# Matmuls without a reader in TensorE's idle places, and modulation sums queued behind named VectorE sums

## The chip, the core and the metric

The kernel runs on one core of a Trainium2 chip. The metric is the device time of one execution in microseconds (us); less is better. Times are medians over several runs. A profile comes from one execution of its own; all positions below are us from the start of its span. Engines: PE is TensorE (PEld its weight loads), DVE VectorE, ACT ScalarE, POOL GpSimd, SP the queue that issues most DMAs.

## What is computed

One layer of a diffusion backbone over 1,024 latent and 128 context tokens of width 1,024, all in float32. Cut to what matters here:

```python
def modulation(cvec, w_ada, b_ada):          # for c and for c_ctx
    m = silu(cvec) @ w_ada + b_ada           # 6 vectors of 1024
    return split(m, 6)                       # sh1, sc1, ga1, sh2, sc2, ga2

h = rmsnorm(x, g1) * (1 + sc1) + sh1
...                                          # in-projection, Fourier mixer, attention, merge -> m
x = x + ga1 * (m @ w_out)
h = rmsnorm(x, g2) * (1 + sc2) + sh2
x = x + ga2 * (square(relu(h @ w_ff1)) @ w_ff2)
y = rmsnorm(x, final_g)
```

## The kernel before

Each float32 matrix product is made of three faster passes: an operand is cast to a rounded high part (ScalarE, `whi`) and the rest is its low part (VectorE, `wlo`, by `sub`), and high x high, high x low and low x high are summed in a PSUM bank. Nine tiles of 128 tokens (eight latent ones, and tile 8 for the context) go through these stages: the head (load x, norms, 72 transposes to channel-major, the modulation vectors of the first norm), the in-projection, Fourier mixer and attention, the output projection (`w_out`, in three groups of three tiles), FF1, FF2. The two feed-forward products use a scheme of seven products (numbered 1 to 7) on halves of the operands instead of eight; `prod` makes one of them.

FF1 runs in 16 blocks `p` of 256 hidden columns. In a block, `step_p1`, `step_p4`, `step_p2`, `step_ctx` (context tile), `step_p6`, `step_p7`, `step_p5` and, a block later, `step_p3` are TensorE's products; `ev_p1`, `ev_p2`, `ev_p6`, `ev_p7`, `ev_c2`, `ev_p3` read them out with sums on VectorE and relu and square on ScalarE. `step_p2` goes on in the bank that `ev_p1` must have read before it. `ff1_load` fetches the next block's weights on SP, `ff1_u` and `ff1_sums` split and add them.

The seam between the last `w_out` group (tiles 6, 7, 8) and FF1 is ordered by hand for TensorE, VectorE, ScalarE and GpSimd (`manual_schedule`, from `ff1_load(0)` to `man.close()`). There block 0 is done in two parts, `RA` (three quarters of the latent tokens, 384 columns) and `RB` (128 columns), because the last latent tiles and the context tile come late: `unit_end` closes the last `w_out` sums, `fin_a` adds them to x, `fin_b` makes the norm's scale, `fin_c` transposes the scaled tile and applies the modulation, `t_hi` and `t_lo` write the operand's halves. The context tile's operand is `cth` (ScalarE) and `ctl` (VectorE).

Everything outside that seam is ordered by a planner that simulates the engines with its own costs. It may also put instructions from behind the seam between those of the seam, and it orders SP's queue throughout.

The modulation vectors of the second norm and gate are made by VectorE and ScalarE beside other work: `mod_step` takes one step of `msteps`: a load of 128 KB of `w_ada` on SP and two VectorE products or accumulations (lines 309 and 311), or, at the end of a block of 256 columns, a transpose and a reduction (320, 321). 40 steps (`MOD_LATE`) are left for FF1. During FF1 the loads alternate between two slots in `zh(15, 2)`, which the seam uses until tile 8 is transposed.

`mmt()` gives one of two PSUM banks for small products, `bank6()` one of six, `gt()` one of six large ones.

Of the kernel before, what the change touches and what calls it, by code (L numbers as in the profile page):

```python
# [14 lines left out]
ALU = mybir.AluOpType  # L15
# [22 lines left out]
CH = 384  # L38
# [20 lines left out]
def backbone_kernel(  # L59
# [25 lines left out]
    nc = tc.nc  # L85
# [37 lines left out]
    def mmt():  # L123
        return pmm.tile([P, 512], F32, tag="mm", name=nm("mm"))
# [31 lines left out]
    ident = const.tile([P, P], F32, name="ident")  # L156
# [5 lines left out]
    cols = const.tile([P, 80], F32, name="cols")  # L162
# [168 lines left out]
    def mod_step(n):  # L331
        for _ in range(n):
            if msteps:
                msteps.pop(0)()

    with ExitStack() as sf:
        qa = sf.enter_context(tc.tile_pool(name="qa", bufs=6, space=PSUM))

        def bank6():
            return qa.tile([P, 512], F32, tag="x", name=nm("x"))  # L340
# [4 lines left out]
        with ExitStack() as s0:  # L345
# [6 lines left out]
            ps = mmt()  # L352
            nc.tensor.transpose(ps[:, :80], rows_sb, ident[:80, :80])
            nc.vector.tensor_copy(cols, ps[:, :80])
            nc.vector.tensor_tensor(pairsum, ident[0:4, 0:4:2], ident[0:4, 1:4:2], ALU.add)
            sl = p0.tile([P, 16], F32, name="sl")
            nc.scalar.activation(sl, cols[:, 0:16], AF.Exp, scale=-1.0)
            warm = p0.tile([P, 1], F32, name="warm")
            nc.scalar.activation(warm, sl[:, 0:1], AF.Sqrt)
# [157 lines left out]
        for gi in range(4):  # L517
# [44 lines left out]
            e = gi % 2  # L562
# [602 lines left out]
    def fin_c(t, kh):  # L1165
        tok = 0 if t < 8 else 1
        px = mmt()
        hn, yt = XS[t % 3], ys[t]
        for q in range(4):
            nc.tensor.transpose(px[:, q * P : (q + 1) * P], hn[:, (kh * 4 + q) * P : (kh * 4 + q + 1) * P], ident)  # L1170
        for q in range(4):
            k = kh * 4 + q
            src = px[:, q * P : (q + 1) * P]
            if kh == 0:
                nc.scalar.activation(yt[:, k], src, AF.Identity, bias=mod(3, k, tok), scale=s2[:, k, tok : tok + 1])
            else:
                nc.vector.tensor_scalar(yt[:, k], src, s2[:, k, tok : tok + 1], mod(3, k, tok), ALU.mult, ALU.add)
# [74 lines left out]
    def unit_end(t, h):  # L1252
        wout_mm(b3[t, h], t, h, *last[1])
# [15 lines left out]

    R4 = (0, 4)  # L1270

    def prod(ps, p, i, r=R4, cont=False):
        t0, tn = r
        po = ps[:, : tn * P].rearrange("p (t c) -> p t c", t=tn)
        for k, ((wh, wl), (xh, xl)) in enumerate(zip(wsel(p, i), T[i])):
            xh, xl = xh[:, t0 : t0 + tn], xl[:, t0 : t0 + tn]
            nc.tensor.matmul(po, wh, xh, start=(k == 0 and not cont), stop=False, skip_group_check=cont)  # L1277
            nc.tensor.matmul(po, wh, xl, start=False, stop=False, skip_group_check=cont)  # L1278
            nc.tensor.matmul(po, wl, xh, start=False, stop=(k == 3), skip_group_check=cont)  # L1279
# [4 lines left out]
    def win(x, r):  # L1284
        return x[:, : r[1] * P]
# [4 lines left out]
    def relu2(v):  # L1290
        nc.scalar.activation(v, v, AF.Relu)
        nc.scalar.activation(v, v, AF.Square)

    def step_p1(p, r=R4):
        s_ = st[p, r] = {"a": gt()}
        prod(s_["a"], p, 1, r)

    def ev_p1(p, r=R4):
        s_ = st[p, r]
        s_["u2"] = obuf(p, r, 0)  # L1300
        nc.scalar.copy(s_["u2"], win(s_["a"], r))  # L1301

    def step_p2(p, r=R4):
        prod(st[p, r]["a"], p, 2, r, cont=True)
# [38 lines left out]

    def ev_p6(p, r=R4):
        s_ = st[p, r]
        nc.vector.tensor_tensor(s_["u2"], win(s_["b"], r), s_["u2"], ALU.add)

    def step_p7(p, r=R4):
        st[p, r]["c"] = gt()
# [7 lines left out]
    def ev_c2(p, r, half, keep):  # L1357
        s_ = st[p, r]
        v = obuf(p, r, 3) if keep else s_["u3"]
        nc.vector.tensor_tensor(v, win(s_["d" if half else "e"], r), s_["u3"], ALU.add)  # L1360
        relu2(v)

    def step_p5(p, r=R4):
        st[p, r]["d"] = gt()
# [57 lines left out]
    wu[0][2] = tuple(map(k4, u2))  # L1422
    for h in range(2):
        unit_end(8, h)
    step_p1(0, RA)
    ev_p1(0, RA)
    step_p2(0, RA)
    fin_b1(6, 2)
    u3 = uhi(zh(9, 2))
# [46 lines left out]
    step_p5(0, RB)  # L1476
    step_p6(0, RB)
    ev_p6(0, RB)
    fin_c(8, 0)
    fin_c(8, 1)  # L1480
    step_p2(0, RB)
# [54 lines left out]
    def pre_prep():  # L1536
# [6 lines left out]
        load_hc(2, hc_tile("whi"))  # L1543
        load_hc(3, hc_tile("wlo"))

    for p in range(1, NPR):
        if p == 1:
            ff1_u(p, 2)
        step_p1(p)
        ev_p1(p)  # L1550
        step_p4(p)
        if p > 1:
            step_p3(p - 1)
            ev_p3(p - 1)
            del wu[p - 1]
        ff1_sums(p)
        step_p2(p)
        ev_p2(p)
        if p + 1 < NPR:
            ff1_load(p + 1)  # L1560
        else:
            pre_load()
        step_ctx(p)
        step_p6(p)
        ev_p6(p)
        store_57(p - 1)
        step_p7(p)
        ev_p7(p)
        store_63(p - 1)
        ev_c2(p, R4, 0, True)  # L1570
        store_first(p, 1)
        store_first(p, 2)
        if p + 1 < NPR:
            ff1_u(p + 1, 1)
        else:
            pre_prep()
        step_p5(p)
        ev_c2(p, R4, 1, False)
        store_first(p, 4)
        if p + 1 < NPR:  # L1580
            ff1_u(p + 1, 2)
        step_ctx2(p)
        if 1 < p < 15:
            mod_step(3)
        if p == 14:
            mod_step(len(msteps))
            mod_fold()
            ga_rows(5, 2)
# [334 lines left out]
```

## Time and profile before

| | us |
|---|---|
| median of 3 runs | 1704.21 (1703.84 to 1704.77) |
| profiled execution | 1705.88 |
| its span | 1703.7 |
| TensorE busy in the span | 1639.0 (96%) |
| VectorE | 1189.6 (70%) |
| ScalarE | 904.7 (53%) |
| GpSimd | 293.9 (17%) |

The span is what the trace covers; the 2.2 us between it and the profiled execution's time lie around it. Busy shares are means over stages with different limits, so the stage in question has to be looked at by itself.

### The profile page before, as it was taken

Reading aid. Unit: us, or ns where it says so; the run is one execution under the profiler, and the core shown is the slowest. Engines: PE = TensorE matmul, PEld = TensorE weight load, DVE = VectorE, ACT = ScalarE, POOL = GpSimd, SP = SyncE. Lnnn points to the kernel's source line nnn. Section 1 sums busy time; section 2 is a strip of 40 time slices with the busy share of each in tenths; the row PEclk is TensorE's granted clock in tenths of the full one; section 3 lists DMA queues with packets and bytes.
Section 4 is the critical chain, followed back from the end, with each engine's and each line's share of the span. In section 5 each row is a group of like instructions: output and inputs, shape, how many; then the busy total and the mean of one; then the engine's idle time right before and its main releaser. Section 6 shows DMA issues by size and latency. Waiting matters only on the chain.

```text
span 1703.7 us, 26341 instructions
## 1 busy us (share of the span) xinstructions
PE 1639.0 (96%) x9025; PEld 1453.9 (85%) x9025; DVE 1189.6 (70%) x2408; ACT 904.7 (53%) x1826; POOL 293.9 (17%) x374
## 2 busy tenths in 40 slices
PE   6999999999999999899999899999999999999997
PEld 5799889999899899799987788888888888888886
DVE  7653247778778877778757978668666488876764
ACT  6443236766767777655436644544444354444542
POOL 3410004435435444300001400000000200000000
PEclk9999999999999999999999889999999999999999
DMA  9342491223322311279555535444444996666751
GB/s 299 112 132 69 136 246 52 80 71 80 98 67 79 92 58 51 95 246 307 182 203 180 160 98 181 167 149 153 163 142 154 281 386 217 198 190 192 249 160 62
DMA packets 219222, 265.57 MB, mean 156 GB/s; under 512 B 32248, under 2 KB 148920, under 8 KB 219088
## 3 DMA queue, kind: packets, MB, share of 16 engines
q1 hardware_dynamic: 210832, 253.93, 46.9%
q0 software_dynamic: 8256, 9.96, 2.2%
q8 instruction: 71, 1.16, 0.3%
q14 instruction: 63, 0.52, 0.1%
HBM read 195.38 MB, written 68.44 MB: 155 GB/s over the span
## 4 chain that ended last, share of the span: by engine, by line
PE 67%; DVE 11%; DMA 7%; ACT 6%; issue 3%; POOL 2%; SPq 0%; DVEq 0%; ACTq 0%; POOLq 0%
PE x L1666 6%; PE x L1667 6%; PE x L1668 6%; PE x L1277 6%; PE x L1279 6%; PE x L1278 6%; DVE pt L712 2%; PE mm L192 2%; PE mm L193 2%; PE mm L194 2%; PE ptp L753 2%; PE x L192 1%; ACT pt L724 1%; PE x L194 1%; PE x L193 1%
## 5 line engine op out<-in xcount | busy, mean ns | idle before, releaser
L139 DVE TENSOR_TENSOR wlo<-wraw,whi 128x1024 fp32r<-128x1024 f32 x100 | 126.3, 1265 | 83.4 <-ACT whi L144 83.1
L144 ACT CAST whi<-wraw 128x1024 fp32r<-128x1024 f32 x98 | 102.5, 1049 | 105.3 <-PE x L232 22.7
L1667 PE MATMUL x<-BR 128*128 128x512 f32 x336 | 130.7, 389 | 0.0
L1668 PE MATMUL x<-BR 128*128 128x512 f32 x336 | 130.2, 389 | 0.0
L1666 PE MATMUL x<-BR 128*128 128x512 f32 x336 | 129.0, 389 | 0.0
L734 POOL TENSOR_SCALAR pt<-pt,mx 128x512 f32<-128x512 f32 (+2 forms) x144 | 96.8, 684 | 159.0 <-DVE mx L732 142.6
L724 ACT ACTIVATE pt<-pt,mx 128x513 f32<-128x513 f32 (+2 forms) x144 | 94.7, 660 | 33.5 <-DVE mx L722 32.9
L712 DVE CUSTOM_DVE_ANT_0 pt<-s,mask,sink 128x512 f32<-128x512 f32 (+2 forms) x144 | 94.7, 672 | 20.9 <-PE ptp L753 11.4
L1639 ACT CAST BR<-aa 128x512 fp32r<-128x512 f32 x80 | 49.7, 621 | 104.5 <-PE x L1667 50.3
L139 DVE TENSOR_TENSOR pl<-ptp,ph 128x512 fp32r<-128x512 f32 (+1 forms) x136 | 86.1, 640 | 15.8 <-ACT ph L758 14.7
L304 POOL TENSOR_TENSOR macc<-macc,mprod 128x512 f32<-128x512 f32 x70 | 92.3, 1319 | 20.4 <-ACT mprod L302 20.2
L193 PE MATMUL mm<-BR,whi 128*128 128x384 f32 x272 | 91.9, 338 | 0.0
L758 ACT CAST ph<-ptp 128x512 fp32r<-128x512 f32 (+1 forms) x136 | 72.5, 546 | 31.3 <-PE ptp L753 29.7
L1277 PE MATMUL x<-BR,whi 128*128 128x512 f32 (+2 forms) x204 | 81.3, 398 | 6.4 <-ACT ZR L1301 3.8
L192 PE MATMUL mm<-BR,whi 128*128 128x384 f32 x240 | 83.4, 348 | 0.0
L194 PE MATMUL mm<-BR,wlo 128*128 128x384 f32 x240 | 81.2, 338 | 0.0
L1279 PE MATMUL x<-BR,wlo 128*128 128x512 f32 (+2 forms) x204 | 79.9, 392 | 1.1 <-DVE wlo L139 1.1
L1278 PE MATMUL x<-BR,whi 128*128 128x512 f32 (+2 forms) x204 | 79.6, 390 | 0.0
L753 PE MATMUL ptp<-ident,pt 128*128 128x128 f32 x496 | 76.0, 274 | 2.7 <-ACT qT L694 2.1
L139 DVE TENSOR_TENSOR BR<-aa,BR 128x512 fp32r<-128x512 f32 x80 | 55.0, 687 | 29.0 <-ACT BR L1639 28.4
L302 ACT ACTIVATE mprod<-mraw,siluc 128x256 f32<-128x256 f32 x140 | 63.8, 502 | 21.0 <-POOL macc L304 20.5
L1668 PEld LDWEIGHTS x<-BR 128*128 128x128 f32 x336 | 63.1, 188 | 13.2
(460 smaller groups left out, 5206.8 us busy)
## 6 DMA issues: line engine op xcount, KB each, us to landing
aa<-hr_d SPq DMA_DIRECT2D x108, 256.0 KB
ab<-in_w_ff_dram SPq DMA_DIRECT2D x108, 256.0 KB
hr_d<-ZR SPq DMA_DIRECT2D x104, 256.0 KB
wraw<-in_w_in_dram SPq DMA_DIRECT2D x40, 512.0 KB
wraw<-in_w_ff_dram SPq DMA_DIRECT2D x34, 512.0 KB
mraw<-in_w_ada_dram SPq DMA_DIRECT2D x96, 128.0 KB
wraw<-in_w_out_dram SPq DMA_DIRECT2D x24, 512.0 KB
z_d<-z SPq DMA_DIRECT2D x48, 192.0 KB
```

The costliest lines, as they stand in the source:

```text
L139: eng.tensor_tensor(dst, raw, hi.bitcast(F32), ALU.subtract)
L192: nc.tensor.matmul(out, ah, bh, start=start, stop=False)
L193: nc.tensor.matmul(out, ah, bl, start=False, stop=False)
L194: return nc.tensor.matmul(out, al, bh, start=False, stop=stop).ins
L712: nc.vector.tensor_tensor_reduce(out=pt[:, e, :n], in0=sp[:, :n], in1=mask[:, m0 : m0 + n], scale=1.0, scalar=sink8[:, h0 + e : h0 + e + 1 ...
L724: nc.scalar.activation(pt[:, e, : n + 1], pt[:, e, : n + 1], AF.Exp, bias=mx[:, 2 + e : 3 + e], scale=0.125, accum_out=mx[:, 4 + e : 5 + e],)
L1277: nc.tensor.matmul(po, wh, xh, start=(k == 0 and not cont), stop=False, skip_group_check=cont)
L1278: nc.tensor.matmul(po, wh, xl, start=False, stop=False, skip_group_check=cont)
L1279: nc.tensor.matmul(po, wl, xh, start=False, stop=(k == 3), skip_group_check=cont)
L1666: nc.tensor.matmul(ps, xh, bh, start=start, stop=False, skip_group_check=cont)
L1667: nc.tensor.matmul(ps, xh, bl, start=False, stop=False, skip_group_check=cont)
L1668: nc.tensor.matmul(ps, xl, bh, start=False, stop=stop, skip_group_check=cont)
```

## The change

Four groups of matmuls are added whose result no instruction reads. In the head, 24 products of `ident` with the first 80 columns `cols` are placed in the program between the copy of `cols` and the exponential. In the seam, `warm(n)` makes n products of 384 columns from operand `T[1]` into a small bank: nine before step 1 of block 0's `RA` part, twelve between its `ev_p1` and step 2, seven between the `RB` part's `ev_p6` and the transposes of tile 8.

Second, FF1's modulation steps, three at the end of each of the blocks 2 to 14, become one behind each of three VectorE sums of the block: that of `ev_p6` and the first sums of the two `ev_c2`. `tc.issue_after(ins)` orders what the enclosed code issues on the engine of `ins`, here VectorE, behind `ins` in that engine's queue. Loads on SP and matmuls issued inside it get no such order. The remaining step, the fold and the gate rows stay at the end of block 14.

```diff
             sl = p0.tile([P, 16], F32, name="sl")
+            pw = bank6()
+            for _ in range(24):
+                nc.tensor.matmul(pw[:, :80], ident, cols, start=True, stop=True)
             nc.scalar.activation(sl, cols[:, 0:16], AF.Exp, scale=-1.0)
...
+    def warm(n):
+        ps, (a, b) = mmt(), T[1][0]
+        for _ in range(n):
+            nc.tensor.matmul(ps[:, :CH], a[:, 0], a[:, 0:3], start=True, stop=True)
...
     def ev_p6(p, r=R4):
         s_ = st[p, r]
-        nc.vector.tensor_tensor(s_["u2"], win(s_["b"], r), s_["u2"], ALU.add)
+        return nc.vector.tensor_tensor(s_["u2"], win(s_["b"], r), s_["u2"], ALU.add).ins
...
-        nc.vector.tensor_tensor(v, win(s_["d" if half else "e"], r), s_["u3"], ALU.add)
+        ins = nc.vector.tensor_tensor(v, win(s_["d" if half else "e"], r), s_["u3"], ALU.add).ins
         relu2(v)
+        return ins
...
     for h in range(2):
         unit_end(8, h)
+    warm(9)
     step_p1(0, RA)
     ev_p1(0, RA)
+    warm(12)
     step_p2(0, RA)
...
     step_p6(0, RB)
     ev_p6(0, RB)
+    warm(7)
     fin_c(8, 0)
...
+    def mod_behind(p, ins):
+        if 1 < p < 15:
+            with tc.issue_after(ins):
+                mod_step(1)
+
     for p in range(1, NPR):
...
-        ev_p6(p)
+        mod_behind(p, ev_p6(p))
...
-        ev_c2(p, R4, 0, True)
+        mod_behind(p, ev_c2(p, R4, 0, True))
...
-        ev_c2(p, R4, 1, False)
+        mod_behind(p, ev_c2(p, R4, 1, False))
...
         step_ctx2(p)
-        if 1 < p < 15:
-            mod_step(3)
         if p == 14:
```

## Rows read from the trace of the kernel before

**Rows 1.** The page, the span in 40 equal slices: TensorE's busy share and its granted clock, both in tenths (9 is 90% or more).

```profile
PE   6999999999999999899999899999999999999997
...
PEclk9999999999999999999999889999999999999999
```

**Rows 2.** The table by stage: stretch and its length, busy us and instructions of TensorE, its weight loads, VectorE, ScalarE and GpSimd, granted clock (1.00 is full), share of the DMA engines, GB/s.

```profile
12.40:18.00 5.60, 5.38 (x24) 4.98 (x24) 4.57 (x12) 5.04 (x12) 2.11 (x2) 1.00 1.12 346
...
960.00:1012.00 52.00, 41.94 (x224) 39.40 (x225) 41.71 (x88) 30.40 (x64) 6.48 (x4) 0.77 0.32 102
1012.00:1320.00 308.00, 308.00 (x1531) 260.85 (x1530) 215.57 (x332) 143.36 (x224) 0.79 (x1) 1.00 0.47 158
```

**Rows 3.** Waits of TensorE from 958 to 1012 us: what waited, for whom, us in total, times, longest.

```profile
PE x L1277 <- ACT ZR L1301: 3.8, 1, 3.8
PE x L1277 <- DVE ZR L1125: 2.4, 1, 2.4
PE mm L1170 <- ACT ZR L1158: 1.7, 1, 1.7
PE x L1279 <- DVE wlo L139: 1.1, 1, 1.1
```

**Rows 4.** The table by stage again, in slices of 2 us, where the granted clock falls.

```profile
962.00:964.00 2.00, 1.60 (x8) 1.63 (x9) 1.93 (x4) 0.63 (x2) 1.92 (x2) 0.86 0.04 8
...
994.00:996.00 2.00, 2.00 (x13) 2.00 (x12) 1.79 (x6) 1.58 (x5) 0.00 (x0) 0.54 0.38 124
```

**Rows 5.** TensorE in order of time in the seam: start, duration (matmuls overlap, so a pace is the distance of starts), line, output, inputs, shape, and in brackets the idle time before it and its releaser. L1277 to L1279 are `prod`, L1322 to L1324 `step_ctx`, L1170 `fin_c`.

```profile
962.40 0.41 PE L1277 MATMUL x<-BR,whi 128*128 128x384 f32 x1 [2.43 <-DVE ZR L1125]
...
969.57 0.69 PE L1277 MATMUL x<-BR,whi 128*128 128x384 f32 x1 [3.84 <-ACT ZR L1301]
...
973.58 0.39 PE L1277 MATMUL x<-ER,whi 128*128 128x384 f32 x1
...
979.50 0.42 PE L1277 MATMUL x<-ER,whi 128*128 128x384 f32 x1
...
981.67 0.33 PE L1277 MATMUL x<-BR,whi 128*128 128x384 f32 x1
...
988.02 0.28 PE L1277 MATMUL x<-ER,whi 128*128 128x128 f32 x1
...
989.36 0.28 PE L1277 MATMUL x<-ER,whi 128*128 128x128 f32 x1
...
992.59 1.09 PE L1170 MATMUL mm<-ident,ZR 128*128 128x128 f32 x8 [1.72 <-ACT ZR L1158]
...
995.96 0.41 PE L1277 MATMUL x<-ER,BT 128*128 128x128 f32 x1
...
998.51 0.41 PE L1277 MATMUL x<-BR,whi 128*128 128x128 f32 x1
...
1002.11 0.58 PE L1324 MATMUL mm<-whi,BT 128*128 128x256 f32 x1 [0.30 <-DVE BT L139]
...
1006.97 0.31 PE L1277 MATMUL x<-ER,BT 128*128 128x128 f32 x1
...
1011.76 0.50 PE L1279 MATMUL x<-BR,wlo 128*128 128x512 f32 x1 [1.05 <-DVE wlo L139]
...
1014.20 0.28 PE L1323 MATMUL mm<-wlo,BT 128*128 128x256 f32 x1
...
1015.62 0.40 PE L1277 MATMUL x<-ER,whi 128*128 128x512 f32 x1
```

**Rows 6.** VectorE and ScalarE in the seam. First VectorE's groups of instructions from 996 to 1012 us (line, operation, shapes, count, busy us, mean ns, idle us before them and releaser), then single entries in order of time: `ev_p1` (ACT L1301), the low part for step 6, accumulations with their wait, `ctl` (with a second subtraction joined to it), accumulations, and the low part of block 1's first weights.

```profile
L311 DVE SCALAR_TENSOR_TENSOR ZR<-ZR,siluc 128x256 f32<-128x256 f32 x14 | 6.2, 480 | 3.0 <-DMA ZR<-in_w_ada_dram 3.0
...
L309 DVE TENSOR_SCALAR ZR<-ZR,siluc 128x256 f32<-128x256 f32 x2 | 0.6, 349 | 0.2 <-DMA ZR<-in_w_ada_dram 0.2
...
969.06 0.46 ACT L1301 COPY ZR<-x 128x384 f32<-128x384 f32 x1
...
971.01 1.23 DVE L139 TENSOR_TENSOR wlo<-ZR,whi 128x1024 fp32r<-128x1024 f32 x1
...
999.45 1.27 DVE L311 SCALAR_TENSOR_TENSOR ZR<-ZR,siluc 128x256 f32<-128x256 f32 x3 [0.87 <-DMA ZR<-in_w_ada_dram]
...
1000.84 1.82 DVE L139 TENSOR_TENSOR BT<-ZR,BT 128x1024 fp32r<-128x1024 f32 x2
...
1009.36 0.88 DVE L311 SCALAR_TENSOR_TENSOR ZR<-ZR,siluc 128x256 f32<-128x256 f32 x2 [0.66 <-DMA ZR<-in_w_ada_dram]
...
1010.52 1.18 DVE L139 TENSOR_TENSOR wlo<-wraw,whi 128x1024 fp32r<-128x1024 f32 x1
```

**Rows 7.** The head in order of time: TensorE's transpose of the 80 rows, the first and the second group of transposes of x, and ScalarE's cast of a part of `w_ada`.

```profile
3.72 0.36 PE L353 MATMUL mm<-ident,rows_sb 80*128 80x80 f32 x1 [3.72 <-DMA rows_sb<-in_rows_dram]
12.47 5.38 PE L406 MATMUL x<-ident,xt 128*128 128x128 f32 x24 [8.38 <-DVE xt L401]
18.66 2.81 PE L406 MATMUL x<-ident,xt 128*128 128x128 f32 x24 [0.81 <-DVE xt L401]
...
23.94 1.05 ACT L144 CAST whi<-wada 128x1024 fp32r<-128x1024 f32 x1 [0.77 <-DMA wada<-in_w_ada_dram]
```

**Rows 8.** Block 2's first weights: VectorE's low part, and TensorE's first matmul with them.

```profile
1024.85 1.22 DVE L139 TENSOR_TENSOR wlo<-wraw,whi 128x1024 fp32r<-128x1024 f32 x1
...
1030.30 0.48 PE L1277 MATMUL x<-BR,whi 128*128 128x512 f32 x1
```

## The prediction

> **What bounds the kernel now.** I began with the page's slices of the span [rows 1]: TensorE is busy in nearly every slice after the first, so a gain must come from places where it idles or runs slowly. The second row there gives the granted clock: only the two slices before the middle (in this row's slices of 42.6 us, 937 to 1022 us) are visibly below full. The table by stage [rows 2] narrows it: from 1012 to 1320 us TensorE is busy for 308.00 of 308.00 us at clock 1.00, while from 960 to 1012 us, the seam between the output projection and FF1, it is busy for 41.94 of 52.00 us at a mean clock of 0.77. FF1 is thus bound by TensorE; the seam by whatever hands TensorE its operands, and partly by the clock. Whatever brings the first unbroken stretch (it starts at 1011.76 us, [rows 5]) forward moves the end by as much.
>
> Third, who ends TensorE's waits in the seam [rows 3]: ScalarE's copy for step 2 (3.8 us), VectorE's read of a bank (2.4 us), the scaling of the last token tile (1.7 us), and VectorE's low part of FF1's first weights (1.1 us). Fourth, the clock beside those waits: it falls in 962 to 964 us, behind the 2.43 us wait, and in 994 to 996 us, behind the 1.72 us wait [rows 4, 5]. It does not fall behind the 1.05 us wait before 1011.76. The durations say what half clock (1.2 GHz instead of 2.4) costs: 12 matmuls of 384 columns take 4.01 us (969.57 to 973.58) against 2.17 us (979.50 to 981.67); 12 of 128 columns 2.55 us (995.96 to 998.51) against 1.34 us (988.02 to 989.36); 256 columns 0.22 us each (1002.11 to 1006.97, 22 of them) against 0.12 us (1014.20 to 1015.62, 12 of them) [rows 5].
>
> **The change, part by part.** *Head, 24 matmuls of 80 columns.* They need cols, which needs the transpose at 3.72 us and a copy that ends about 4.4 us. Their pace is not in the trace: at least 0.117 us (the transposes at full clock, 2.81 us for 24), at most 0.36 us (the 80-column transpose) [rows 7]. Nearest is the first group of transposes with the same stationary size, 5.38 us for 24, so 0.22 us each: they run from 4.4 to 9.8 us, all inside the 8.38 us wait before 12.47. At 0.36 us they would end at 13.0 and push the first transposes by 0.6 us: the loss bound. The gain bound: that group at 2.81 us instead of 5.38 us would free its evictions 2.6 us earlier, of which the next group, which starts at 18.66 behind VectorE, could use some 1.2 us, an estimate. I take 0.2 us, because TensorE still stands idle from 9.8 to 12.47 us, longer than the 2.43 us after which the clock fell in the seam, and because ScalarE's cast at 23.94 waits 0.77 us for w_ada, which no matmul brings closer while the DMA engines' share is 1.12 [rows 2, 7].
>
> *warm(9), before step 1.* 9 x 0.18 = 1.6 us in a gap of 2.43 us. Worth nothing by itself: step 1 ends at 965.73 (969.57 less its 3.84 us wait) and ScalarE copies the result only at 969.06, for its queue stands behind squares that wait for VectorE [rows 5, 6]. At half clock it would be 9 x 0.33 = 3.0 us, 0.6 us over the gap, hidden by that slack of 3.3 us.
>
> *warm(12), before step 2.* If step 1 is at full clock it ends at 964.6, and the 12 (2.2 us) at 966.8. TensorE then still waits 2.8 us for the copy at 969.06. That is longer than the gap that brought the clock down, so I don't count on step 2 at full speed. At full speed it would take 2.17 us instead of 4.01, less some 0.2 us in which step 6 waits for the low part made from 971.01 to 972.24 [rows 6]: 1.6 us. At half clock throughout the 12 take 4.0 us and end at about 969.7: 0.2 us lost. Between -0.2 and 1.6 I take 0.6, step 2 partly slow.
>
> *warm(7), before the last tile's transposes.* 7 x 0.18 = 1.3 us in the 1.72 us gap before 992.59: 0.4 us remain, under the 1.05 us that the clock survived, then 1.09 us of transposes. I expect full clock. Then steps 2, 7 and 4 of the narrow part (36 matmuls from 993.7) end at 997.7 instead of 1001.1.
>
> *The sums.* mod_behind orders only what it issues on VectorE; the loads of w_ada stay on SP's queue as before. In the seam VectorE now does 14 accumulations of 0.48 us and 2 products of 0.35 us and waits 3.2 us for their loads [rows 6]. None of it can stand there any more: the first is ordered behind step 6 of block 2. Two places were on TensorE's path. First ctl, which TensorE awaits until 1002.11: ahead of it stand 0.87 us of waiting and 1.27 us of accumulation (999.45), and before that two products and two accumulations (1.3 us with overlap). Without these 3.4 us ctl would start at 997.4, but its other half cth must be cast first, which I put at 997.7 (step 2's result is read 0.9 us earlier): ctl ends at 998.9. Second, the low part of FF1's first weights at 1010.52, which stands behind a wait of 0.66 us, 0.88 us of accumulation and a transpose: 1.5 us late.
>
> So the context step: its third matmul at 998.9 instead of 1002.11, the other 22 at 0.118 us, end 1001.7 instead of 1007.1: 5.4 us. The clock alone would give 2.2 (ctl still late), the sums alone some 0.75 (steps at half clock until 1001.1). Then relu, square, cast and the low part as before, but 1.4 of the 1.5 us sooner.
>
> *Where the sums go.* 39 steps, three a block, in blocks 2 to 14, about 3 x 0.96 us of VectorE in a block of some 21.4 us. Cost zero: TensorE covers it (308.00 of 308.00), and the same work stands in blocks 1 to 8 now without a wait of TensorE. If that cover were gone: the next weights' low part is ready at 1026.07, TensorE takes it at 1030.30 [rows 8], so 4.2 us of slack.
>
> **Sum.** 0.2 + 0 + 0.6 + 5.4 + 1.4 = 7.6 us. The profiled execution took 1705.88 us with a span of 1703.7, so 1698.3 with a span of 1696.1; the median of the runs is 1.67 us under the profiled one, so 1704.2 - 7.6 = 1696.6.
>
> **Rivals.** *The clock falls again in the narrow part* (warm(7) too short, or the remaining gap longer because TensorE arrives earlier). For: behind the gap come the same transposes and matmuls in which it fell. Against: only 0.4 us of idle is left. It gives 0.2 + 0.6 + 0.75 + 1.5 = 3.1 us: 1701.1.
>
> The Trainium skill (TensorE: Matmul & The Clock Gate, Part 1) says that the moment at which the clock changes differs from run to run of the same kernel. By that rule the term of 0.6 would be anything from -0.2 to 1.6 in each execution, and this rival could hold in some executions and not in others. No run here shows it: one trace, and three times within 0.93 us.
>
> *It doesn't do what it says.* The planner that orders everything outside the hand-ordered seam fills VectorE's freed time with other sums or reorders the head around the new matmuls, and TensorE waits as long for something else. Against: the other VectorE work of 1003 to 1007 us is some 3 us and fits. It gives about 1703.5.
>
> *Slower.* SP's queue is in order. A w_ada load waits there for its slot, that is for an accumulation that now stands behind a sum of its block, and FF1's next weights behind it. A third of a block is 7.1 us; less the slack of 4.2 us that is 2.9 us per block. It decides from the third such block (8.7 us against 7.6); in four of them 11.6 us: 1708.2. Against: the planner orders SP with the sums' new places before it.
>
> **Chances.** Forecast 0.55; clock falls again 0.20; no effect 0.13; slower 0.12. What a measurement here can tell from no change is 0.2%, 3.4 us. Faster than that: all of the first and two fifths of the second, 0.63; same: the rest of the second and all of the third, 0.25; slower 0.12. The forecast's own range, from the bounds (head -0.6 to 1.2, step 2 -0.2 to 1.6, and 1 us either way for the planner), is 1694.2 to 1699.3. For 8 in 10 it reaches over the second case and into the third: 1694.0 to 1703.3.
>
> **What would show it.** After: no clock below 1.00 from 984 to 1012 us; step 2 at 0.18 or 0.33 us a matmul; the context step over by about 1002 us; no modulation sum on VectorE before block 2's step 6; the unbroken stretch from about 1004.5 us; TensorE without idle time after it. Wrong, if the narrow part is still slow, if TensorE waits in blocks 2 to 14 for weights, or if the head moves by over 1 us.

## The result, and the profile of the changed kernel

The changed kernel is slower: a median of 1709.72 us (1707.80 to 1714.15) against 1704.85 us of the kernel before in the same session; the ratio is 1.0025, 95% interval 1.0014 to 1.0035, or +4.3 us (2.4 to 6.0) where -7.6 us was forecast. The medians of the kernel before lie between 1704.85 and 1708.33 us from session to session, so every kernel is compared with it by the ratio of the two in one session. The profiled execution of the changed kernel took 1714.15 us, the slowest of its runs, with a span of 1712.4 us; a second profiled execution (below, h4) took 1708.58 us, beside 1710.24 us of one execution of the kernel before.

I read the new trace by position: for the same instruction of TensorE, how much later it stands than before. This table is worked out from starts and ends of landmarks in the two traces.

```
position before, us        103    315    702    752    960   1334   1351    end
first profile, later by   +2.3   +4.2   +4.5  +12.1  +10.7   +3.4   +8.8   +8.8
second profile, later by  +3.2   +4.0   +2.6   +4.7   +4.4   -2.2   +3.2   +3.2
```

The seam (960 to 1012 us) gives back 7.1 and 6.5 us, nearly as forecast. Three bills stand against it: some 3 us in the head, a changing amount between 103 and 752 us, and 5.4 us around 1343 us, where FF1 ends and FF2 begins.

**The seam.** The page's slices and the table by stage of the changed kernel (the seam lies 10 us later, 970 to 1022 us):

```profile
PE   8999999999999999899999999999999899999997
...
PEclk9999999999999999999999999999999999999999
```

```profile
970.00:1022.00 52.00, 46.62 (x289) 43.00 (x289) 41.74 (x79) 32.54 (x67) 6.52 (x4) 0.97 0.29 99
1022.00:1330.00 308.00, 308.00 (x1526) 260.86 (x1525) 218.52 (x345) 143.59 (x226) 2.42 (x4) 1.00 0.48 162
1330.00:1360.00 30.00, 25.58 (x118) 20.88 (x117) 9.97 (x18) 7.97 (x14) 4.81 (x7) 0.94 0.95 250
```

The mean granted clock of the seam went from 0.77 [rows 2] to 0.97, and the 1.7 us wait for the last tile [rows 3] to 0.4. But in the slice from 1330 to 1360 us TensorE is idle for 4.4 of 30 us. In order of time (L1278 is `warm`, L1285 `prod`, L1173 `fin_c`, L1332 the part of `step_ctx` that needs ctl):

```profile
970.51 1.75 PE L1278 MATMUL mm<-BR 128*128 128x384 f32 x9
...
974.61 2.25 PE L1278 MATMUL mm<-BR 128*128 128x384 f32 x12
...
979.64 0.44 PE L1285 MATMUL x<-BR,whi 128*128 128x384 f32 x1 [2.78 <-ACT ZR L1309]
...
982.61 0.52 PE L1285 MATMUL x<-ER,whi 128*128 128x384 f32 x1
...
1000.51 1.45 PE L1278 MATMUL mm<-BR 128*128 128x384 f32 x7
1002.37 1.10 PE L1173 MATMUL mm<-ident,ZR 128*128 128x128 f32 x8 [0.42 <-ACT ZR L1161]
1003.50 0.33 PE L1285 MATMUL x<-BR,whi 128*128 128x128 f32 x1
...
1009.17 0.39 PE L1332 MATMUL mm<-whi,BT 128*128 128x256 f32 x1 [0.75 <-DVE BT L139]
...
1011.78 0.28 PE L1332 MATMUL mm<-whi,BT 128*128 128x256 f32 x1
```

Step 2 starts after ScalarE's copy as before and takes 2.97 us instead of 4.01, since the clock falls within it (0.87 from 978 to 982 us, 0.71 from 982 to 986); behind `warm(7)` it holds, at 1.00 from 1000 to 1022 us. The context step's last product starts 2.61 us after the first that needs ctl, 21 products later: 0.12 us each instead of 0.22 [rows 5].

**From FF1 to FF2.** TensorE's only wait there before, then its waits in the changed kernel from 1325 to 1365 us, ScalarE's, and the stretch behind them in the table by stage:

```profile
1343.27 0.44 PE L1334 MATMUL mm<-ident,ZR 128*128 128x128 f32 x2 [0.98 <-ACT ZR L1327]
```

```profile
PE mm L1342 <- ACT ZR L1335: 3.3, 1, 3.3
PE mm L1681 <- DMA whi<-hc_d: 1.2, 1, 1.2
```

```profile
ACT BR L1529 <- DMA wraw<-in_w_ff_dram: 11.1, 1, 11.1
```

```profile
1350.00:1354.00 4.00, 4.00 (x13) 3.16 (x12) 2.31 (x4) 2.68 (x5) 0.00 (x0) 0.63 1.18 389
```

TensorE's last context transposes (L1342) wait for ScalarE's square (L1335); the relu and the square stand on ScalarE's queue behind a cast (L1529, FF2's first weights) that waits 11.1 us for its load. The 5.4 us are mostly three parts: this wait is 2.3 us longer than before, the wait for the load of `hc_d` (1.2 us) is new, and from 1350 to 1354 us the clock is at 0.63, which costs some 1.5 us (an estimate: 0.37 of 4 us). ScalarE in order of time, before (L1517) and after (L1529), and what SP issued, before and after:

```profile
1341.34 1.14 ACT L1517 CAST BR<-wraw 128x512 fp32r<-128x512 f32 x2 [8.81 <-DMA wraw<-in_w_ff_dram]
```

```profile
1347.05 1.14 ACT L1529 CAST BR<-wraw 128x512 fp32r<-128x512 f32 x2 [11.11 <-DMA wraw<-in_w_ff_dram]
```

```profile
1321.19 1.01 SPq L941 DMA_DIRECT2D ga_d<-mods  x2
...
1330.66 0.38 SPq L1532 DMA_DIRECT2D wraw<-in_w_ff_dram  x1
```

```profile
1333.02 1.03 SPq L944 DMA_DIRECT2D ga_d<-mods  x2
1334.28 0.39 SPq L1544 DMA_DIRECT2D wraw<-in_w_ff_dram  x1
```

`ga_rows(5, 2)`, the two writes of the gate vectors, needs the last modulation sums. Those now end with block 14, so the fold and the writes moved from 9.5 us ahead of FF2's load to 1.3 us ahead of it. What the writes do shows in the table by stage, the ten microseconds after them, before and after (the last two columns are the DMA engines' share and GB/s), and in the count of packets, after, from 1333 to 1346 us:

```profile
1322.00:1332.00 10.00, 10.00 (x49) 8.43 (x48) 4.29 (x6) 5.38 (x10) 2.10 (x4) 1.00 1.00 33
```

```profile
1336.00:1346.00 10.00, 9.70 (x49) 7.93 (x47) 1.00 (x2) 0.00 (x0) 3.07 (x5) 1.00 0.67 56
```

```profile
DMA packets 2442, 0.83 MB, mean 64 GB/s; under 512 B 2107, under 2 KB 2107, under 8 KB 2442
```

The writes are 8 KB in 2,048 elements. Of the 2,107 small packets 2,094 lie between 1333 and 1336 us; the slow time comes behind them, for about 10 us at 33 to 56 GB/s in both kernels, in the changed one although FF2's load waits there. Before, most of that time was over when the load was issued. Counted from a load's issue to the start of the cast that waits for it, which I call its landing from here on, the load took 10.7 us before and 12.8 us after.

**The head.** TensorE in order of time (L359 are the added products, L409 the transposes):

```profile
3.68 10.53 PE L359 MATMUL x<-cols,ident 128*128 128x80 f32 x48 [0.33 <-DVE cols L354]
13.99 6.24 PE L409 MATMUL x<-ident,xt 128*128 128x128 f32 x36
```

Each of the 24 products leaves two entries of 0.22 us, that is 0.44 us for a product: 10.5 us instead of the 5.4 that I reckoned, and the transposes of x start at 13.99 instead of 12.47 us [rows 7]. The trace of the kernel before already had this, for the two float32 products of its line 446:

```profile
30.85 0.60 PE L446 MATMUL mm<-pairsum,mr 4*128 4x2 f32 x4 [0.45 <-ACT mr L442]
```

Nor did the products bring the quick pace forward. By the starts of the single transposes TensorE, busy since 3.68 us, makes one in 0.22 us up to 18.05 us and in 0.11 us from 18.43 us on; before, the change lies between 17.22 and 18.80 us. The granted clock can't be read that early: the trace's first entry for it is at 18.4 us (17.9 us before), and up to there the tables show 1.00 for want of an entry, in [rows 2] too.

### The profile page after: what moved, and what is told of

Same layout as the page of the kernel before. It is cut to its first block, busy times and chain, and to the rows that moved or that the text cites. A ratio compares the mean times of both kernels' runs of the same rounds, so it can differ in the third digit from the quotient of the medians.

```text
span 1712.4 us, 26474 instructions
## 1 busy us (share of the span) xinstructions
PE 1653.8 (97%) x9101; PEld 1466.6 (86%) x9101; DVE 1185.7 (69%) x2408; ACT 902.5 (53%) x1826; POOL 295.3 (17%) x374
## 4 chain that ended last, share of the span: by engine, by line
PE 75%; DVE 8%; DMA 4%; ACT 4%; issue 3%; POOL 1%; SPq 0%; DVEq 0%; ACTq 0%; POOLq 0%
PE x L1683 6%; PE x L1682 6%; PE x L1681 6%; PE x L1285 5%; PE x L1287 5%; PE x L1286 5%; PE mm L192 3%; PE mm L193 2%; PE mm L194 2%; PE x L192 2%; PE x L193 2%; PE x L194 2%; PE ptp L756 2%; PE x L1117 1%; PE x L1118 1%
## 5 line engine op out<-in xcount | busy, mean ns | idle before, releaser
L1285 PE MATMUL x<-BR,whi 128*128 128x512 f32 (+2 forms) x204 | 79.5, 390 | 3.4 <-ACT ZR L1309 2.8
L1286 PE MATMUL x<-BR,whi 128*128 128x512 f32 (+2 forms) x204 | 77.9, 382 | 0.0
L1299 ACT ACTIVATE ZR<-ZR 128x512 f32<-128x512 f32 (+2 forms) x51 | 30.8, 603 | 85.4 <-DVE ZR L1368 78.2
```

## The experiments

Four theories: the **rows** theory (the gate rows' writes, now directly ahead of FF2's load, cost the 5.4 us), the **head** theory (the 24 matmuls cost what the trace shows at 103 us), its wider form (they also cost something later, in the attention), and chance of the clock. A time named for a kernel is its difference to the kernel before, by the measured ratio, with the 95% interval.

### One part at a time

The head's matmuls alone (e1), the three `warm` groups alone (e2), the sums alone (e3).

> The kernel before with the 24 matmuls of the head alone. Theory 1 (three bills: the changed trace is 2.3 us late at 103 us, after the head; another 9.7 us late at 749 us; and 5.3 us late from FF1 to FF2, against 7.6 us gained in the seam): the planner orders the head anew around the 24 matmuls, so this kernel carries the first bill, 2.3 us, and, as the order of instructions from 103 to 960 us is the same in both, the second bill is the clock's and differs from execution to execution: 2 to 3 us slower than before. Rival (the shifted head moves the attention, and the waits of 0.85 to 1.38 us at 720 to 745 us are its systematic result): 6 to 12 us slower, with the loss again between 715 and 752 us. Rival 2 (the head's loss is chance): no difference.

> The kernel before with the three groups of matmuls in the seam alone. Theory 1: the clock part of the seam, 2.2 us for the narrow part and up to 1.6 us for step 2, while ctl stays late: 2 to 4 us faster, nothing lost in the head or from FF1 to FF2. Rival (the matmuls only fill the waits and the clock falls anyway): no difference, or up to 1 us slower.

> The kernel before with the modulation sums one behind each named sum alone. Theory 1: the seam gains 0.75 to 3 us, because the narrow part still runs at half clock; from FF1 to FF2 5.3 us are lost, because the sums end at about 1327 us and the gate rows' writes stand directly ahead of FF2's first weights: 2 to 5 us slower than before. Rival (the loss from FF1 to FF2 is the clock's fall, not the rows'): 1 to 3 us faster, with no wait of ScalarE's cast of over 9 us for the weights near 1340 us.

e1: +2.0 us (0 to 4.1). e2: -3.1 us (-4.4 to -1.5). e3: +2.2 us (-0.3 to 5.0), by itself not clear of no difference. TensorE's wait in the head of e1 with the stretch behind it in the table by stage, then TensorE's waits of e2 in the seam and of e3 from FF1 to FF2:

```profile
PE mm L449 <- ACT mr L445: 2.7, 1, 2.7
```

```profile
33.00:36.00 3.00, 2.71 (x14) 2.70 (x15) 2.56 (x4) 0.57 (x2) 2.63 (x2) 0.66 0.93 254
```

```profile
PE mm L1329 <- DVE BT L139: 1.7, 1, 1.7
PE x L1284 <- DVE wlo L139: 1.2, 1, 1.2
```

```profile
PE mm L1334 <- ACT ZR L1327: 8.7, 1, 8.7
```

In e1 TensorE is 3.0 us late at 103 us: the planner put ScalarE's and VectorE's norm work in another order around the longer stretch of products, and behind a 2.7 us wait for a row of the modulation (`mr`) the clock falls to 0.66, where it stood at 1.00 before. In e2 the clock in the seam is 0.93 and the narrow part is fast, but ctl and the low part of FF1's first weights are late as before (the two lines), and behind the wait for ctl the clock falls again, to 0.78 from 1000 to 1003 and 0.65 from 1003 to 1006 us: the seam gains 2.8 us. In e3 the narrow part is slow, but both of these waits are gone: the seam gains 3.2 us, and 9.8 us are lost from FF1 to FF2, with an 8.7 us wait where 0.98 stood; FF2's load lands 17.8 us after its issue there. Clock and sums together gain 6.5 to 7.1 us in the seam, a little more than 2.8 + 3.2.

### The gate rows

e4 moves the writes in the program from block 14 into FF2's loop; e7 does that, without the head's matmuls, and queues them on SP behind a named load; e5 is the changed kernel without the head's matmuls; e6 is the kernel before with only the fold and the writes late.

```diff
# e4, e7: in FF2's loop instead of block 14
+        if s == 12:
+            with tc.issue_after(lastw[0]):   # e7 alone: the last load of w_ff2
+                ga_rows(5, 2)
# e6, on the kernel before: block 15, behind block 14's last sum
+            ins = ev_p3(p - 1)
+            if p == NPR - 1:
+                with tc.issue_after(ins):
+                    mod_fold()
...
+        with tc.issue_after(one(0)):         # FF2's first load
+            last = ga_rows(5, 2)
+        with tc.issue_after(last):
+            one(2)                           # FF2's second load
```

> The changed kernel, but the gate rows (two writes of 1,024 separate elements) are placed in FF2's twelfth step instead of block 14. Theory 1: the writes no longer stand ahead of FF2's first weights, so the 5.3 us from FF1 to FF2 come back: about 5 us faster than the changed kernel, the same as before within 2 us. Rival (the loss is the late fold or the clock): as the changed kernel, 4 us slower than before. Rival 2 (the writes collide with FF2's loads instead): waits of TensorE in FF2's first block, and no gain.

> The changed kernel without the head's 24 matmuls. Theory 1 (the head's bill is its own): about 2.5 us faster than the changed kernel, that is 0 to 2 us slower than before, with the position at 103 us as before and the loss from FF1 to FF2 unchanged at 5 us or more. Rival (the head is chance): as the changed kernel, 4 us slower than before.

> The kernel before, in which only the last fold and the two writes of the gate rows are moved: the fold stands on VectorE behind block 14's last sum (the one of step 3, at 1328.55 us before) and the writes directly ahead of FF2's second load of first weights; all other instructions of all engines keep their order, two neighbours of FF2 apart. Theory 1 (writes of 4-byte elements block the DMA engines for about 10 us, and directly ahead of the 512 KB load they make FF2's weights late): 4 to 9 us slower than before, with ScalarE's cast waiting for those weights for over 10 us and TensorE idle for 3 us or more between 1340 and 1352 us. Rival (the writes cost nothing, something else in the changed order does): within 1 us of before.

> The changed kernel without the head's matmuls and with the gate rows' writes held on SP's queue behind a load of FF2's twelfth step (the earlier try put them late in the program and the planner issued them at 1325 us all the same). Theory 1: seam gain kept, nothing lost from FF1 to FF2: 6 to 8 us faster than before. Rival (the late fold, or the sums of block 14, hold up the transition whatever the rows do): no faster than the kernel without the head's matmuls, TensorE idle near 1343 us as before. Rival 2 (the writes now make FF2's loads late): idle time of TensorE in FF2 of some 5 us, and 0 to 2 us faster than before.

e4: +4.1 us (2.2 to 6.0), where no difference to before was expected. SP's queue in e4:

```profile
1325.29 1.00 SPq L944 DMA_DIRECT2D ga_d<-mods  x2
1326.55 0.65 SPq L1544 DMA_DIRECT2D wraw<-in_w_ff_dram  x1
```

Here the planner issued the writes as soon as the fold was done, although they stand in FF2; a place in the program is no place on SP. The loss was 5.6 us again.

e6: +5.5 us (3.4 to 7.7). SP, the stretch behind it in the table by stage, and TensorE's wait:

```profile
1328.76 1.02 SPq L941 DMA_DIRECT2D ga_d<-mods  x2
1330.02 1.34 SPq L1534 DMA_DIRECT2D wraw<-in_w_ff_dram  x1
```

```profile
1330.00:1340.00 10.00, 10.00 (x57) 8.77 (x56) 2.67 (x4) 1.23 (x2) 3.38 (x5) 1.00 0.68 26
```

```profile
PE mm L1335 <- ACT ZR L1328: 5.2, 1, 5.2
```

TensorE's order is that of the kernel before but for two small products of the fold and two neighbours in FF2, and the loss is there, 6.3 us in the trace: the late fold with the late writes suffices. e7: -7.2 us (-9.2 to -5.1). With the writes at 1384.82 us, after FF2's first loads, no wait of TensorE is left near 1343 us (a wait of 1.6 us at 1438 us is new). SP's load and ScalarE's cast in e7:

```profile
1322.26 0.38 SPq L1541 DMA_DIRECT2D wraw<-in_w_ff_dram  x1
```

```profile
1326.30 1.14 ACT L1526 CAST BR<-wraw 128x512 fp32r<-128x512 f32 x2 [2.37 <-DMA wraw<-in_w_ff_dram]
```

The fold is still at the end of block 14, and on ScalarE the cast still stands ahead of the relu and the square; what is new is that the load lands 4.0 us after its issue. e5 differs from e7 in the writes alone and loses 5.9 us from FF1 to FF2 in its trace. So it is the writes ahead of the load, and not the late fold or ScalarE's order by itself, that cost the time. e5: -5.8 us (-8.5 to -3.2). That is better than the -1 us of seam and transition together; its trace is 3.7 us early at 960 us, more than any other, and why stays open.

### Earlier sums, and rows that are contiguous

e8 takes four sums a block, so that the writes fall into block 12. e9 leaves the writes directly ahead of FF2's load but turns the vectors first; h6 is e9 measured once more.

```diff
# e9, e10 to e12, h1 to h3, h5, h6
-            nc.sync.dma_start(ga_d[row + tok].rearrange("(m p) -> p m", p=P), mods[:, k * 8 : k * 8 + 8, tok])
+        nc.tensor.transpose(pt[:16, :P], mods[:, k * 8 : k * 8 + 8, :].rearrange("p m t -> p (m t)"), ident)
+        nc.vector.tensor_copy(quads[:16], pt[:16, :P])
+            nc.sync.dma_start(ga_d[row + tok].rearrange("(m p) -> m p", p=P), quads[tok:16:2])
```

> The changed kernel without the head's matmuls, with four sums a block instead of three (the second of them behind the last named sum), so that the sums, the fold and the gate rows' writes are over in block 11, where the DMA engines have time. Theory 1: 6 to 8 us faster than before. Rival (four sums a block are too many for VectorE or for SP's queue): waits of TensorE for weights in blocks 2 to 11, and less than 4 us faster.

> The changed kernel without the head's matmuls; the gate vectors are turned by one transpose into rows, so that the two writes before FF2 go out as 8 pieces of 512 bytes each instead of 1,024 of 4, at the same place on SP's queue, directly ahead of FF2's second load of first weights. Theory 1 (it is the 4-byte pieces that hold up the DMA engines): no stretch of 10 us at under 60 GB/s, nothing lost from FF1 to FF2, 7 to 10 us faster than before. Rival (the late fold holds up SP's queue, whatever the size of the pieces): the weights again land after 1345 us, TensorE idles 3 us or more, and about 3 us faster than before.

> The kernel of the transposed rows without matmuls in the head once more: 7 to 11 us faster than before if the first measurement (ratio 0.9946, interval 0.9934 to 0.9958) holds. If it comes out near 4 us, the difference to the kernels with the head's matmuls was chance of these runs.

e8: -4.6 us (-6.5 to -2.9), less than the 6 to 8 expected. VectorE and SP carry four sums a block without a wait of TensorE; the one that it has in blocks 2 to 14 is the writes' again. They went out in block 12, one block later than expected, and now FF1's own weights stand behind them: that load lands 13.3 us after its issue, ScalarE's queue stands behind its cast, and behind TensorE's wait the clock is 0.66 from 1272 to 1276 us. SP, the table by stage and TensorE's wait in e8:

```profile
1256.33 1.00 SPq L941 DMA_DIRECT2D ga_d<-mods  x2
1257.58 0.37 SPq L1077 DMA_DIRECT2D wraw<-in_w_ff_dram  x1
```

```profile
1255.00:1265.00 10.00, 10.00 (x58) 8.76 (x57) 5.13 (x10) 4.68 (x7) 0.00 (x0) 1.00 0.36 12
```

```profile
1272.28 0.44 PE L1339 MATMUL mm<-ident,ZR 128*128 128x128 f32 x2 [3.26 <-ACT ZR L1332]
```

e9: -9.2 us (-11.3 to -7.2), and -10.1 us (-12.1 to -8.0) the second time (h6). SP, the ten microseconds behind it, and ScalarE's cast in e9:

```profile
1326.87 1.44 SPq L950 DMA_DIRECT2D ga_d<-quads  x2
1328.36 0.44 SPq L1551 DMA_DIRECT2D wraw<-in_w_ff_dram  x1
```

```profile
1330.00:1340.00 10.00, 10.00 (x46) 8.17 (x45) 3.35 (x6) 2.87 (x6) 1.84 (x3) 1.00 1.18 366
```

```profile
1336.26 1.14 ACT L1536 CAST BR<-wraw 128x512 fp32r<-128x512 f32 x2 [6.60 <-DMA wraw<-in_w_ff_dram]
```

The writes stand directly ahead of the load as before, but the DMA engines move 366 GB/s behind them instead of 26 to 56; the load lands 7.9 us after its issue (8.6 in h6) instead of 12.8 to 17.8 in the kernels with late 4-byte writes (the changed one, e3 to e6). So the slow time belongs to the 4-byte pieces.

That TensorE loses nothing here has another reason, though. In e9 the planner put the context's relu and square ahead of the waiting cast on ScalarE, so TensorE makes its context transposes before the load has landed:

```profile
1334.32 0.38 PE L1349 MATMUL mm<-ident,ZR 128*128 128x128 f32 x2
```

In the changed kernel these transposes start 1.9 us after the cast (1347.05 to 1348.97 us). In that order they would have started at 1338.2 us here, a wait of 3.9 us (an estimate) against 3.3 in the changed kernel. For in e9 the load is issued 4.4 us behind the square that precedes these steps on ScalarE (at 1323.97 us), in the changed kernel 1.0 us ahead of it (1335.31). So contiguous rows were not shown to save TensorE's time by themselves, and the old order on ScalarE with them was not run. That the place of the 4-byte writes decides rests on e6 and e7, and on e8, where the wait went with the writes.

The packets of e9 from 1326 to 1338 us:

```profile
DMA packets 2169, 4.29 MB, mean 358 GB/s; under 512 B 172, under 2 KB 188, under 8 KB 2169
```

The Trainium skill (DMA: Bandwidth & Descriptors, Rules for kernel authors) says that a strided last dimension lowers to one descriptor per element and should be rearranged to be contiguous. The traces agree: 2,107 packets under 512 B behind the writes of the changed kernel, 172 here.

### More matmuls ahead of step 2

> The kernel of the transposed rows with 24 instead of 12 matmuls ahead of step 2, which fill the 2.8 us that TensorE still waits there for ScalarE's copy. If the clock then holds through step 2, its 12 matmuls take 2.2 us instead of the 4.0 of the half clock: up to 1.8 us faster than with 12. If step 6 then waits for its own operand, or the clock falls all the same: no difference.

-10.4 us (-12.6 to -8.2), against -9.2 and -10.1 with 12: not told apart. TensorE in order of time in e11 (L1285 is `warm`):

```profile
962.27 4.33 PE L1285 MATMUL mm<-BR 128*128 128x384 f32 x24
967.34 0.44 PE L1292 MATMUL x<-BR,whi 128*128 128x384 f32 x1 [0.75 <-ACT ZR L1316]
```

Step 2 and what follows up to 994 us is 1.5 us faster, against 0.3 us in e9. But with 12 products e7 and h5 gained as much (1.5 and 1.6 us): their clock stayed at 1.00. And e4 and h1 lost 0.9 us there, where the clock is 0.66 over ten microseconds (from 968 and from 970 us).

### The head's matmuls

e10 is e9 with the 24 products of the head, e12 with 10 of them, h5 with 10 that write into a free part of the bank of the transposed rows; h1 and h2 are e12 once more, h3 is e10, h4 the changed kernel.

> The kernel of the transposed rows with the head's 24 matmuls in it again. Theory A (the head costs the 2 to 3 us by which it is late at 103 us): 2 to 3 us slower than the kernel without them, 5 to 7 us faster than before. Theory B (the later head also brings out waits and a fallen clock in the attention's end near 715 to 752 us): 5 to 10 us slower than without them.

> The kernel of the transposed rows with 10 matmuls in the head instead of 24 or none. The trace shows each of the 24 as two entries of 0.22 us, 10.5 us in all, ending at 14.0 us, 1.5 us after the time at which the first transposes started before; 10 of them would end at about 8.1 us, before that time. Theory A (the head's loss is the length of the 24): no loss against the kernel without them. Theory B (it is the order in which the planner puts ScalarE's and VectorE's work of the head around them): again 2 to 3 us late at 103 us.

> The kernel of the transposed rows with 10 matmuls in the head that write into the free part of the bank of the transposed 80 rows. If the shifted banks were the cause: as without the matmuls, about 9 us faster than before. If the matmuls themselves are: 4 us faster than before, as with 10 matmuls in a bank of their own.

> A further look at the kernel with transposed rows and 10 matmuls in the head. Theory B (the head's matmuls bring out waits near 700 to 752 us): the clock falls below 0.9 somewhere there and the position at 752 us is 3 us or more behind that at 690 us. Rival (chance of one execution): the stretch as in the first look, under 0.5 us lost in it.

> The kernel with transposed rows and 10 matmuls in the head a third time. The theories expect the same as of the second look: 3 us or more lost from 690 to 752 us, or under 0.5 us.

> A further look at the kernel with transposed rows and 24 matmuls in the head. Theory B: again about 6 us lost between 700 and 752 us (first look: 5.9 at 702 us, 12.05 at 752 us, behind the kernel before). Rival: nothing lost there this time.

> A further look at the changed kernel itself. Theory B: late by 2 to 3 us at 103 us and by 7 or more from 700 to 752 us as in its first profile, and by 5 us from FF1 to FF2. Rival: the loss near 700 to 752 us is gone, the one from FF1 to FF2 stays.

e10: -2.7 us (-4.3 to -1.4), 6.5 us slower than e9. e12: -4.1 us (-5.8 to -2.2), 5.1 us slower than e9. h5: -4.4 us (-6.3 to -2.4), 5.6 us slower than h6 on the same chip. Single times: h1 1702.26, h2 1703.00, h3 1702.68, h4 1708.58 us, beside 1710.24 us of the kernel before; with one execution each, 10 and 24 products aren't told apart here. TensorE in the head of e12:

```profile
3.73 4.55 PE L359 MATMUL x<-cols,ident 128*128 128x80 f32 x20 [0.33 <-DVE cols L354]
11.80 4.92 PE L409 MATMUL x<-ident,xt 128*128 128x128 f32 x24 [3.52 <-DVE xt L404]
```

Ten products end at 8.3 us, in the idle time. They leave the order on TensorE and SP as it is in e9, and on VectorE and ScalarE up to small swaps, which two traces of one kernel (e9 and h6) show as well; TensorE is not late at 103 us. Yet the runs are 5 us slower, and h5 shows that the shift of the banks is not the reason. How much later TensorE stands than in the kernel before, as means over the traces with none (ten, that of before among them), 10 (e12, h1, h2, h5) and 24 (after, e1, e4, e10, h3, h4) products in the head:

```
position before, us     103     315     623     702     752     960
none                   -0.2    -0.4    -1.2    -0.8    -0.7    -0.9
10                     -0.4    +0.5    +0.5    +2.0    +2.8    +3.3
24                     +2.9    +3.8    +3.2    +3.3    +7.0    +6.6
```

Behind these means the single traces spread widely: at 752 us from -3.7 to +1.3 us with none, +0.1 to +5.0 with 10, +0.6 to +12.1 with 24. The 24 cost 3 us in the head. Beyond 103 us, 10 and 24 cost 3.7 to 4.6 us more than none up to 752 us, in small waits at changing places and falls of the clock. It shows best from 710 to 760 us, where the attention ends: TensorE is busy there for 48.8 to 49.3 of 50 us in each of the ten traces without products in the head, and for 46.7 to 48.6 us in each of the ten with them. Since the later traces have somewhat other work in that stretch, I also took it by the same instructions: there the ten without lose -0.1 to +0.4 us against the kernel before, the ten with products 0.9 to 7.6. The expectations of h1 to h4 named 3 us or more (h1, h2), 6 (h3) and 7 (h4), or nothing; from 690 to 752 us h1 lost 2.0 and h2 3.3 us, from 702 to 752 us h3 and h4 2.2 us. The extremes, from 740 to 750 us in the table by stage, before and in the changed kernel:

```profile
740.00:750.00 10.00, 10.00 (x58) 8.73 (x58) 4.13 (x6) 3.83 (x11) 0.00 (x0) 1.00 0.88 268
```

```profile
740.00:750.00 10.00, 8.10 (x33) 6.63 (x33) 6.46 (x16) 3.70 (x8) 1.03 (x2) 0.77 0.49 155
```

So the wider head theory holds as a fact and not as a mechanism: why products that run in idle time 700 us earlier bring this out stays open. No run tells, for one, whether it is their work or only that TensorE's program is longer by them. Nor do the comparisons agree on its size: e1 gives 2 us, e10, e12 and h5 5.1 to 6.5, the changed kernel against e5 10 us, the last from two different sessions.

## Why the prediction was wrong

By measured parts the sum is: seam -7.0, FF1 to FF2 +5.4, head +6, together about +4.4 us, beside +4.3 measured. That it comes so close is luck: the head's 6 us is chosen from comparisons that give 2 to 10. Without the head's products, and with no loss from FF1 to FF2, e9 and h6 are 9.2 and 10.1 us faster, somewhat more than the 7.4 us forecast for the seam.

- **Seam: right.** Forecast 0.6 + 5.4 + 1.4 = 7.4 us; 6.4 to 7.1 us in the changed kernel (twice), e5, e9 and h6, 7.7 to 8.5 where step 2 ran at full clock (e7, e11, h5), 5.1 and 5.3 where the clock stayed low for longest behind step 1 (e4, h1). The context step came 5.3 us nearer (9.8 to 4.5 us late between 993.7 and 1008.7), the low part of FF1's first weights 1.0 us. Clock alone 2.2 + 0.6 forecast, 2.8 measured (e2); sums alone 0.75 + 1.5 forecast, 3.2 measured (e3).
- **Step 2: right in its doubt, with too narrow bounds.** 0.6 forecast between -0.2 and 1.6. Of fifteen traces with the 12 products eleven got 0.2 to 0.5, e7 and h5 1.5 and 1.6, and e4 and h1 lost 0.9, which is below the lower bound. One and the same kernel gained 0.3 us in e12 and h2 and lost 0.9 in h1. That the moment at which the clock changes differs between runs of one kernel is what the Trainium skill (TensorE: Matmul & The Clock Gate, Part 1) says, and these traces agree.
- **"Where the sums go. Cost zero": the step that failed.** The slack of TensorE in blocks 2 to 14 was real (e8 shows four sums a block without a wait of its own). But the step costed only VectorE's time of the sums. It did not follow what waits for the *last* of them: the fold, behind it two writes with 10 slow microseconds of the DMA engines, behind these on SP's queue FF2's first weights, and behind their cast on ScalarE the relu and square that TensorE awaits. Price 5.4 us, and 6.3 us when only this was done (e6). The rival of SP's queue named the right queue and the wrong transfers: behind w_ada's loads TensorE has no wait, 308.00 of 308.00 us busy from 1022 to 1330 us.
- **Head 0.2 us: mis-sized, and the wrong way.** The pace of 0.22 us was right per entry, but each product makes two, 0.44 us where 0.36 was the upper bound, so they end at 14.2 us and not at 9.8. That and the planner's new order around them cost 3 us, and no gain came, since the transposes' quick pace began no earlier; the rest of some 6 us was no term at all, and its cause is open. The statement that the head would not move by over 1 us was the sign that failed first.
- The lower end of the forecast's own range, 1694.2, does not follow from the bounds named for it: 1696.6 less 1.0 (head), 1.0 (step 2) and 1.0 (planner) is 1693.6. The result lies far above the upper end, so nothing hangs on it.
- The rival that the clock falls again in the narrow part did not come in the changed kernel: it is at 1.00 from 1000 to 1012 us, behind `warm(7)`. In e2, where ctl is still late, it fell in the context step.

## What to carry to other kernels

When work is spread later behind named instructions, follow the last piece to its consumers and to every queue that these stand in, not only the time of the pieces: here the end of a sum decided when two tiny writes went out. Vectors written across partitions, element by element, were 8 KB with 10 slow microseconds of the DMA engines behind them; one transpose ahead of the writes took these away. Look also at what stands on an engine's queue behind the instruction that awaits a late load: in e9 two short instructions moved ahead of it were enough to spare TensorE the wait. And fill an idle place only where the clock behind it matters and is seen to fall: the seam's 28 products gained, the head's 24 gained nothing and cost twice.

## What the runs showed of the hardware

- Behind two writes of 1,024 elements of 4 bytes the DMA engines move 12 to 56 GB/s for about 10 us, though nearly all the small packets are over in the first 3 us. A 512 KB load issued right behind them lands after 12.8 to 17.8 us; behind 16 pieces of 512 bytes it lands after 7.9 and 8.6 us, and after 4.0 us with the writes elsewhere (e7).
- A float32 product of 80 columns leaves two entries of 0.22 us each (48 for 24 products); a transpose of the same stationary size leaves one.
- With TensorE busy from 3.68 us on, its transposes in the changed kernel keep the pace of 0.22 us up to 18.05 us and have 0.11 us from 18.43 us on.
- Of the planner, not of the chip: in e4 it issued the writes at 1325 us although they stand in FF2 in the program; in e7 an order on the issuing queue itself held them back.
- Ten products without a reader at 4 to 8 us made the whole run 5 us slower (e12 and h5), with the order on TensorE and SP unchanged; the cause is open.
